# Hybrid S5 and stick-breaking layer: one weight sum of a Strassen-Winograd group moved to an adding DMA, and six more such groups

## The chip, the cores and the metric

The kernel runs on one core of one Trainium2 chip. The metric is the device time of one execution in microseconds (us), the median of several runs. A profiled execution of the same program gives the trace that is read here.

## The reference, cut to what matters

One layer for 256 positions of width 2048: a half feed-forward (FFN 1), a mixer (state space and attention), a second half feed-forward (FFN 2) and a per-layer embedding. All numbers are float32. The change touches the two feed-forwards only, each with its own weights:

```python
def swiglu(h, w_gate, w_up, w_down):
    return (jax.nn.silu(h @ w_gate) * (h @ w_up)) @ w_down
x = x + 0.5 * swiglu(rms_norm(x, ffn1_norm[i]), ffn1_w_gate[i], ffn1_w_up[i], ffn1_w_down[i])
```

The gate and up weights are 2048 x 5632 and the down weight is 5632 x 2048, so one FFN streams 138 MB of weights through the core for 256 rows of activations.

## The kernel before, in words

**Products in three passes.** TensorE multiplies float32r (a rounded form of float32). Each operand is split into a high part and a low rest, and a product is hi x hi, lo x hi and hi x lo, three matmuls of 128 x 128 by 128 x 512. A weight tile `raw` holds four K tiles of 128 rows by 512 columns (1 MB) and comes by a DMA of the SP queue; there are five such buffers. `split` (L181, L184) turns half of it, 128 x 1024 elements, into a pair: ScalarE casts the high part (`whi` or `shi`), VectorE subtracts to get the rest (`wlo` or `slo`).

**Plain blocks and columns.** `gemm_block` and `Seven.column` take a weight tile half by half: one pair and twelve matmuls (two K tiles, two row tiles of 128 positions, three passes) into two PSUM banks.

**Groups of seven.** `Seven.chunk` (L505) takes two weight tiles at once (in the gate and up stage one of `w_gate` and one of `w_up`, in the down stage two neighbouring column blocks) and forms a Strassen-Winograd product of 2 x 2 blocks. The weight blocks are b11 and b21 (the halves of the first tile) and b12 and b22 (the halves of the second). `Seven.add` (L500, recorded at L502) forms four sums on VectorE: t1 = b11+b12, t2 = t1+b22, t4 = t2+b21, t3 = b12+b22. `Seven.product` (L488, matmuls at L495, L496 and L498) splits one block or sum into a pair and does six matmuls. There are seven products with their own PSUM banks, 42 matmuls where two columns take 48. The matching sums of the activations (`sum_forms`, L459) are made once for each stretch of K.

**Where groups stand.** In the gate and up stage a block f is 512 columns of both weights and has K in four pieces kb = 0 to 3. The flag `two` (L605) chooses: with it, kb 0 and 1 are groups and kb 2 and 3 are columns; without it, only kb 0 is a group. In FFN 2, f = 0 is a plain pair and f = 1 to 10 alternate, starting with `two`. In FFN 1, f = 0 to 6 are plain (the preparation of the state-space part runs beside them), f = 7 (`early`) has one group, and f = 8, 9, 10 have two, one, two. The down stage has three groups in each FFN, by a written plan (L688). This makes 27 groups in all. After a block's last product `opened` and `gated` (L590, L595) fold the banks on VectorE, L621 adds the last one and `turned` transposes.

**The ring of pairs.** `weight_pair` (L284) hands out the buffers: four pairs `whi`/`wlo`, and while `ring` holds a pool, three more (`shi`/`slo`) in turn with them, seven in all. `sums_phase` (L294) fills `ring` when it opens: at the start of FFN 2, and before f = 7 in FFN 1.

**Order.** Each engine executes its own list in order. The order of the lists comes from the framework's planner, which may move an instruction ahead of others that it does not depend on; instructions inside `pin` keep their place. `step` and `put_off` run waiting work between groups of matmuls. SP issues the weight loads and the transposing copies `hT<-mid`; the queue of POOL (GpSimd) carries a few DMAs, among them `fetch_x` (L146, recorded at L150), which brings the residual back into two of the five `raw` buffers near the end of the gate and up stage.

Of the kernel before, what the change touches and what calls it, by code (L numbers as in the profile page):

```python
# [13 lines left out]
ALU = mybir.AluOpType  # L14
# [19 lines left out]
def layer_kernel(ctx: ExitStack, tc: tile.TileContext, a: dict, shapes: dict, out: bass.AP):  # L34
    nc = tc.nc
# [27 lines left out]
    def uid(s):  # L63
        count[0] += 1
        return f"{s}_{count[0]}"
# [4 lines left out]
    def com(tag):  # L70
        return get(comp, tag, *{"sg": (1024, 1), "h": (1024, 2), "sq": (NB, 1), "mid": (2048, 1)}[tag])

    def phase(name):
        return tc.tile_pool(name=name, bufs=1, reuse_waits="tile")
# [24 lines left out]
    def step():  # L99
        for g in list(beside):  # L100
            if next(g, beside) is beside:
                beside.remove(g)

    def finish(g):
        for _ in g:
            pass

    def put_off(steps, fn, *args):


        def g():
            for _ in range(steps):
                yield
            fn(*args)

        return start(g())
# [165 lines left out]
    ring = [None, 0]  # L282
# [10 lines left out]
    @contextmanager  # L293
    def sums_phase(name):  # L294
        with phase(name) as pool:
            ring[:] = [pool, 0]
            yield pool
            ring[0] = None

# [150 lines left out]
    def sum_forms(pool, u, kind="n"):  # L450

        sums = pool.tile([P, 2, NB], F32, tag="sum", name=uid("rows"), bufs=2)
        s = sums.rearrange("p j n -> p (j n)").rearrange("p (z j x b) -> p z j x b", z=4, j=2, b=32)
        (a11, a21), (a12, a22) = ([u[:, k : k + 2, 4 * t : 4 * t + 4] for t in range(TT)] for k in (0, 2))
        for z, (x, y, op) in enumerate((
            (a21, a22, ALU.subtract), (s[:, 0], a11, ALU.subtract),
            (a11, a21, ALU.subtract), (a12, s[:, 1], ALU.add),
        )):
            nc.vector.tensor_tensor(out=s[:, z], in0=x, in1=y, op=op)  # L459
        both = halves(kind)  # L460
        split(*both, sums.rearrange("p j n -> p (j n)").rearrange("p (z t) -> p z t", z=4))
        return both

    class Seven:
# [39 lines left out]

        def chunk(self, kb, final=()):  # L505

            raws = []
            for w, n0 in self.ws:
                raw = wp.tile([P, 4, NB], F32, tag="raw", name=uid("raw"), bufs=5)
                nc.sync.dma_start(  # L510
                    raw, w[4 * kb * P : 4 * (kb + 1) * P, n0 : n0 + NB].rearrange("(j p) n -> p j n", p=P)
                )
                raws.append(raw)
            b11, b21, b12, b22 = (raw[:, 2 * h : 2 * h + 2, :] for raw in raws for h in range(2))
            parts, sums = self.act(kb), self.sums(kb)

            def whole(k, t):
                return [[u[:, 2 * k + j, t * P : (t + 1) * P] for j in range(2)] for u in parts]

            def summed(z):  # L520
                return [[u[:, z, j * P : (j + 1) * P] for j in range(2)] for u in sums]

            self.product(1, whole(0, 0), b11, final)
            t1 = self.add(b11, b12)
            self.product(5, summed(0), t1, final)
            step()
            t2 = self.add(t1, b22)
            self.product(6, summed(1), t2, final)
            t4 = self.add(t2, b21)
            self.product(4, whole(1, 1), t4, final)  # L530
            step()
            t3 = self.add(b12, b22)
            self.product(7, summed(2), t3, final)
            self.product(2, whole(1, 0), b21, final)
            step()
            self.product(3, summed(3), b22, final)
            step()

        def column(self, side, kbs, final=False):
# [14 lines left out]
    def ffn(i, xn, nxt, bg=None):  # L554
# [3 lines left out]
        early = 7 if bg else 0  # L558
# [19 lines left out]
        for f in range(NF):  # L578
            if prep and f == early:
                finish(prep)  # L580
                side.close()
                prep = None
                sevens = pools.enter_context(sums_phase(f"sums{i}"))
                hp = pools.enter_context(phase(f"h{i}b"))
                sums = [sum_forms(sevens, whole_rows(sevens, xn(kb)), "h") for kb in range(2)]
            if sevens and f:
                sg, hh = com("sg"), com("h")
                gate_cols, up_cols = ([u[:, t * NB : (t + 1) * NB] for t in range(TT)] for u in (sg, hh))

                def opened(s, g=gate_cols, u=up_cols):  # L590
                    nc.scalar.copy(g[0], s.bank(1))
                    nc.vector.tensor_tensor(out=u[0], in0=s.bank(6), in1=g[0], op=ALU.add)
                    nc.vector.tensor_tensor(out=u[1], in0=s.bank(7), in1=u[0], op=ALU.add)

                def gated(s, g=gate_cols, u=up_cols, hh=hh):  # L595
                    for z, (ps, other) in enumerate(((s.bank(2), g[0]), (s.bank(4), u[1]))):
                        nc.vector.tensor_tensor(out=g[z], in0=ps, in1=other, op=ALU.add)
                        nc.scalar.activation(g[z], g[z], AF.Silu, scale=xn.rs(z))
                    v = hh.rearrange("p (t n) -> p t n", t=TT)
                    nc.vector.tensor_tensor(  # L600
                        out=v, in0=s.bank(5).unsqueeze(1).to_broadcast([P, TT, NB]), in1=v, op=ALU.subtract
                    )

                s = Seven(xn, lambda kb: sums[kb], ((wg, f * NB), (wu, f * NB)), sevens)
                two = f % 2 == (0 if bg else 1)  # L605
                if f == early:
                    s.column(0, (1, 2, 3))
                    s.chunk(0, (*shared, 2, 4))
                    put_off(0, opened, s)
                elif two:  # L610
                    s.chunk(0)
                    s.column(0, (2, 3))
                    s.chunk(1, (*shared, 2, 4))
                    put_off(0, opened, s)
                else:
                    s.chunk(0, shared)
                    put_off(0, opened, s)
                    s.column(0, (1, 2, 3), True)
                put_off(0, gated, s)
                s.column(1, (2, 3) if two and f != early else (1, 2, 3), True)  # L620
                nc.vector.tensor_tensor(out=hh, in0=s.banks[3.8], in1=hh, op=ALU.add)  # L621
                for t in range(TT):
                    nc.vector.scalar_tensor_tensor(  # L623
                        out=up_cols[t], in0=up_cols[t], scalar=xn.rs(t), in1=gate_cols[t], op0=ALU.mult, op1=ALU.mult
                    )
                put_off(2, turned, hp, f, hh)
                continue

            def gate():
                for t in range(TT):  # L630
                    nc.scalar.activation(sg[:, t * NB : (t + 1) * NB], pg[t], AF.Silu, scale=xn.rs(t))

            first = ()
            if f == 0 and bg:
                warm_up(10)
                first = first_quarters(wg, xn)
            if f == 0 and not bg:
                both = gemm_pair(xn, ((wg, 0), (wu, 0)), KD)
                pg = next(both)
                sums = [sum_forms(sevens, whole_rows(sevens, xn(kb))) for kb in range(2)]  # L640
            else:
                pg = gemm_block(xn, wg, f * NB, KD, first)
            sg = com("sg")
            if f == 0 and bg:
                for n in range(ND):
                    put_off(n, load_x, n)
                    put_off(n + 2, xn.squares, n)
                put_off(6, gate)
            else:
                gate()  # L650
            pu = gemm_block(xn, wu, f * NB, KD) if f or bg else next(both)
            if prep and f == 0:
                start(prep)
            hh = com("h")
            for t in range(TT):
                nc.vector.scalar_tensor_tensor(
                    out=hh[:, t * NB : (t + 1) * NB], in0=pu[t], scalar=xn.rs(t),
                    in1=sg[:, t * NB : (t + 1) * NB], op0=ALU.mult, op1=ALU.mult,
                )
            put_off(2, turned, hp, f, hh)  # L660
# [31 lines left out]
        for n in range(0, ND, 2):  # L692
# [17 lines left out]
            for u in plan:  # L710
                kb, final = int(u[1:]), u == plan[-1]
# [715 lines left out]
    pool = s5p.enter_context(phase("s5"))  # L1427
# [10 lines left out]
    pool = atp.enter_context(phase("attn"))  # L1438
# [105 lines left out]
    early, part, ms, root, r, tmp = (small(1) for _ in range(6))  # L1544
# [132 lines left out]
```

## Time and profile before

| What | us |
|---|---|
| median of 3 runs (lowest to highest) | 1849.53 (1849.49 to 1849.77) |
| profiled execution, its own time | 1849.49 |
| its span, first to last instruction | 1847.7 |
| PE (TensorE matmul) busy | 1835.4 |
| DVE (VectorE) busy | 1462.3 |
| ACT (ScalarE) busy | 1019.6 |
| POOL (GpSimd) busy | 62.1 |

The profiled execution took 1.8 us more than its span; this is what lies before the first and after the last instruction. Busy time of an engine is the union of its instructions. A matmul row lasts longer than the distance to the next one, because matmuls overlap, so the pace is read from start to start. The 16 DMA engines were busy 63.6% of the span with the queue of SP.

### The profile page before, as it was taken

The page shows a single profiled execution, that of the slowest core. Times are in us where ns is not written, and L with a number is a line of the kernel's source. Part 1 is how long each engine was busy: PE and PEld are TensorE (multiplying, and loading weights), DVE is VectorE, ACT ScalarE, POOL GpSimd, SP SyncE. Part 2 cuts the span into 40 slices and gives each one's busy share as a digit, 9 for nine tenths or more (in the row PEclk, how much of TensorE's full clock was granted, in tenths as well). Part 3 has the DMA queues.
Part 4 walks back from the last instruction along what each step waited for, and adds up shares of the span by engine and source line. Part 5 has one row for each costly group of instructions (what it writes and reads, how often), then busy time and mean ns, then how long its engine had stood idle before and what let it go on. Part 6 is the DMA issues. An engine that isn't in the chain of part 4 may idle for free. (4 is left out here: it accounts for less than half of the span.)

```text
span 1847.7 us, 23966 instructions
## 1 busy us (share of the span) xinstructions
PE 1835.4 (99%) x9032; PEld 1518.1 (82%) x9032; DVE 1462.3 (79%) x1718; ACT 1019.6 (55%) x1187; POOL 62.1 (3%) x108
## 2 busy tenths in 40 slices
PE   9999999999999999999999999999999999999998
PEld 7888887788888888888898888888888888888887
DVE  8967664999987976687566799989898998797655
ACT  7444444555565655365685465555555645565554
POOL 0011000000000000010021000000000000000000
PEclk9999999999999999999999999999999999999999
DMA  9888867567656566675636776675656585656563
GB/s 331 284 270 282 251 213 220 182 227 239 229 197 241 187 233 209 192 263 166 216 139 214 219 271 212 226 240 188 205 183 228 200 267 185 247 184 232 179 220 125
DMA packets 232308, 406.36 MB, mean 220 GB/s; under 512 B 26785, under 2 KB 50721, under 8 KB 231905
## 3 DMA queue, kind: packets, MB, share of 16 engines
q1 hardware_dynamic: 227824, 392.81, 63.6%
q0 software_dynamic: 3648, 10.62, 1.8%
q8 instruction: 70, 1.15, 0.3%
q10 hardware_dynamic: 720, 1.41, 0.2%
q14 instruction: 46, 0.37, 0.1%
HBM read 373.46 MB, written 11.93 MB: 209 GB/s over the span
## 5 line engine op out<-in xcount | busy, mean ns | idle before, releaser
L184 DVE TENSOR_TENSOR wlo<-raw,whi 128x1024 fp32r<-128x1024 f32 x473 | 572.3, 1221 | 215.8 <-ACT whi L181 207.4
L181 ACT CAST whi<-raw 128x1024 fp32r<-128x1024 f32 x473 | 491.6, 1051 | 400.6 <-PE acc L324 258.0
L323 PE MATMUL acc<-whi,nhi 128*128 128x512 f32 x1112 | 436.3, 392 | 1.6 <-ACT whi L181 1.6
L324 PE MATMUL acc<-whi,nlo 128*128 128x512 f32 x1112 | 433.2, 390 | 0.0
L328 PE MATMUL acc<-wlo,nhi 128*128 128x512 f32 x1112 | 304.2, 389 | 0.3 <-DVE wlo L184 0.2
L323 PEld LDWEIGHTS acc<-whi,nhi 128*128 128x128 f32 x1112 | 209.0, 188 | 47.1 <-ACT whi L181 2.4
L328 PEld LDWEIGHTS acc<-wlo,nhi 128*128 128x128 f32 x1112 | 208.6, 188 | 44.5 <-DVE wlo L184 1.2
L324 PEld LDWEIGHTS acc<-whi,nlo 128*128 128x128 f32 x1112 | 209.1, 188 | 42.4
L184 DVE TENSOR_TENSOR slo<-raw,shi 128x1024 fp32r<-128x1024 f32 x166 | 202.0, 1217 | 42.4 <-ACT shi L181 42.3
L181 ACT CAST shi<-raw 128x1024 fp32r<-128x1024 f32 x166 | 174.3, 1051 | 110.7 <-PE acc L324 33.4
L181 ACT CAST whi<-sum 128x1024 fp32r<-128x1024 f32 x61 | 64.2, 1053 | 96.8 <-DVE sum L502 80.9
L181 ACT CAST shi<-sum 128x1024 fp32r<-128x1024 f32 x47 | 49.4, 1052 | 72.7 <-DVE sum L502 56.2
L323 PE MATMUL acc<-whi,hhi 128*128 128x512 f32 x216 | 84.1, 389 | 0.0
L324 PE MATMUL acc<-whi,hlo 128*128 128x512 f32 x216 | 84.0, 389 | 0.0
L324 PE MATMUL aux<-whi,hlo 128*128 128x512 f32 x200 | 77.9, 390 | 0.6 <-DVE hlo L184 0.6
L323 PE MATMUL aux<-whi,hhi 128*128 128x512 f32 x200 | 77.8, 389 | 0.0
L184 DVE TENSOR_TENSOR wlo<-sum,whi 128x1024 fp32r<-128x1024 f32 x61 | 74.5, 1221 | 1.9 <-ACT whi L181 1.2
L184 DVE TENSOR_TENSOR hlo<-hT,hhi 128x1024 fp32r<-128x1024 f32 x56 | 68.1, 1217 | 5.9 <-ACT hhi L181 5.7
L181 ACT CAST hhi<-hT 128x1024 fp32r<-128x1024 f32 x56 | 58.7, 1049 | 15.4 <-PE aux L328 13.1
L502 DVE TENSOR_TENSOR sum<-sum,raw 128x1024 f32<-128x1024 f32 x54 | 66.0, 1221 | 1.0
L328 PE MATMUL acc<-wlo,hhi 128*128 128x512 f32 x216 | 65.7, 390 | 0.2 <-DVE wlo L184 0.2
L323 PE MATMUL acc<-shi,hhi 128*128 128x512 f32 x160 | 62.3, 389 | 0.0
(373 smaller groups left out, 3013.7 us busy)
## 6 DMA issues: line engine op xcount, KB each, us to landing
raw<-in_ffn_w_up SPq DMA_DIRECT2D x88, 1024.0 KB, 6.0
raw<-in_ffn_w_down SPq DMA_DIRECT2D x88, 1024.0 KB, 5.1
raw<-in_ffn_w_gate SPq DMA_DIRECT2D x86, 1024.0 KB, 7.0
raw<-in_w_in SPq DMA_DIRECT2D x32, 1024.0 KB, 5.9
raw<-in_w_out SPq DMA_DIRECT2D x16, 1024.0 KB, 5.3
raw<-in_w_ple_gate SPq DMA_DIRECT2D x16, 1024.0 KB, 5.1
hT<-mid SPq DMA_DIRECT2D x160, 64.0 KB, 4.3
h<-mid SPq DMA_DIRECT2D x176, 32.0 KB, 2.7
```

Of the source, the lines that this page charges most:

```text
L181: copy = nc.scalar.copy(hi, src)
L184: nc.vector.tensor_tensor(out=lo, in0=src, in1=hi.bitcast(F32), op=ALU.subtract)
L323: nc.tensor.matmul(ps[t], lhsT=lh, rhs=hi[:, j, cols], start=start and j == 0, stop=False)
L324: nc.tensor.matmul(ps[t], lhsT=ll, rhs=hi[:, j, cols], start=False, stop=False)
L328: nc.tensor.matmul(ps[t], lhsT=lh, rhs=lo[:, j, cols], start=False, stop=stop and j == 1)
L502: nc.vector.tensor_tensor(out=t, in0=x, in1=y, op=ALU.add)
```

## The change

Four things are edited. In `chunk`, t3 = b12+b22 is no longer made by VectorE: POOL issues a DMA that adds b22 to b12 in place (`accum_op`), after t1 has read b12, and product 7 splits b12 itself. The order of the products becomes 1, 5, 6, 4, 2, 3, 7 (it was 1, 5, 6, 4, 7, 2, 3), and t1 is made ahead of product 1. The flag `two` becomes true for every block after `early`: all ten blocks f = 1 to 10 of FFN 2, and f = 8, 9, 10 of FFN 1, have two groups, so there are 33 groups. `ring` is filled by the first group of an FFN instead of by `sums_phase`.

```diff
     def sums_phase(name):
         with phase(name) as pool:
-            ring[:] = [pool, 0]
             yield pool
             ring[0] = None
...
         def chunk(self, kb, final=()):
 
+            if ring[0] is None:
+                ring[:] = [self.pool, 0]
             raws = []
...
+            t1 = self.add(b11, b12)
+            nc.gpsimd.dma_start(b12, b22, accum_op=ALU.add)
             self.product(1, whole(0, 0), b11, final)
-            t1 = self.add(b11, b12)
             self.product(5, summed(0), t1, final)
             step()
             t2 = self.add(t1, b22)
...
             self.product(4, whole(1, 1), t4, final)
             step()
-            t3 = self.add(b12, b22)
-            self.product(7, summed(2), t3, final)
             self.product(2, whole(1, 0), b21, final)
+            self.product(3, summed(3), b22, final)
             step()
-            self.product(3, summed(3), b22, final)
+            self.product(7, summed(2), b12, final)
             step()
...
-                two = f % 2 == (0 if bg else 1)
+                two = f != early
```

## The prediction

> **What bounds the kernel now.** I read the page first, for the shares; then the busy time of each engine in the ten blocks f = 1 to 10 of FFN 2, where five of the six new groups go; then the waits of VectorE there, and single rows.
>
> ```profile
> span 1847.7 us, 23966 instructions
> PE 1835.4 (99%) x9032; PEld 1518.1 (82%) x9032; DVE 1462.3 (79%) x1718; ACT 1019.6 (55%) x1187; POOL 62.1 (3%) x108
> ```
>
> ```profile
> core 0: us, PE busy (x) PEld busy (x) DVE busy (x) ACT busy (x) POOL busy (x), PEclk, DMA share, GB/s
> 1088.70:1129.60 40.90, 40.90 (x182) 33.85 (x182) 40.53 (x40) 23.92 (x26) 0.00 (x0) 1.00 0.58 206
> 1129.60:1171.70 42.10, 42.10 (x187) 34.86 (x186) 34.94 (x34) 22.27 (x24) 0.00 (x0) 1.00 0.69 225
> ...
> 1378.60:1420.70 42.10, 41.80 (x184) 34.12 (x184) 34.06 (x33) 22.79 (x24) 0.00 (x0) 1.00 0.69 225
> 1420.70:1461.60 40.90, 40.90 (x182) 33.49 (x181) 39.98 (x39) 21.55 (x23) 0.00 (x0) 1.00 0.59 206
> 1461.60:1503.70 42.10, 41.91 (x184) 34.11 (x183) 38.18 (x40) 24.96 (x27) 4.33 (x8) 1.00 0.74 234
> sum 415.00, PE 414.51 PEld 341.79 DVE 377.80 ACT 226.82 POOL 4.33; mean PE 41.45 PEld 34.18 DVE 37.78 ACT 22.68 POOL 0.43
> ```
>
> Each window is one block: the 40.90 us ones have two groups, the 42.10 us ones one. PE is busy 414.51 of 415.00 us at clock 1.00, so TensorE bounds this stage and a matmul taken away is time taken away, as long as the pairs arrive. VectorE is the next bound: 40.53 of 40.90 us in a block with two groups, about 35 of 42.10 us in the next one, where it catches up.
>
> ```profile
> DVE sg L597 <- PE acc L328: 13.3, 8, 4.7
> DVE wlo L184 <- ACT whi L181: 9.9, 7, 3.2
> DVE h L621 <- PE aux L328: 8.2, 5, 4.5
> DVE slo L184 <- ACT shi L181: 2.5, 4, 1.4
> DVE hlo L184 <- ACT hhi L181: 1.2, 1, 1.2
> ```
>
> These waits (total, times, longest) make about 35 us of VectorE idle in the ten blocks, and 21.5 us of it are L597 and L621 waiting for PE to finish: VectorE is ahead there. That idle time is the room for more groups.
>
> **The change part by part.** *Fewer matmuls.* The pace of PE comes from two starts:
>
> ```profile
> 1088.74 0.39 PE L495 MATMUL acc<-whi,hhi 128*128 128x512 f32 x1
> 1094.18 0.39 PE L495 MATMUL aux<-whi,nhi 128*128 128x512 f32 x1
> ```
>
> The second is four products (24 matmuls) behind the first: 5.44 / 24 = 0.227 us each, 1.36 us for a product. A new group replaces two columns, 42 matmuls for 48, so it saves 1.36 us. Six groups (five in FFN 2, one in FFN 1's f = 9) save 36 matmuls, 6 x 1.36 = 8.2 us, all on the path.
>
> *VectorE.* Its pace also comes from starts:
>
> ```profile
> 1227.90 1.21 DVE L184 TENSOR_TENSOR slo<-raw,shi 128x1024 fp32r<-128x1024 f32 x1
> 1229.04 1.21 DVE L184 TENSOR_TENSOR wlo<-raw,whi 128x1024 fp32r<-128x1024 f32 x1
> 1230.17 1.21 DVE L184 TENSOR_TENSOR slo<-raw,shi 128x1024 fp32r<-128x1024 f32 x1
> 1231.31 1.21 DVE L184 TENSOR_TENSOR wlo<-raw,whi 128x1024 fp32r<-128x1024 f32 x1
> ```
>
> Three steps in 3.41 us are 1.14 us for an operation of 128 x 1024. A group had 7 subtractions and 4 sums; now it has 7 and 3. Two columns have 4 subtractions. In the ten blocks of FFN 2, 15 old groups lose one sum each and 5 new ones add 10 - 4 = 6 each: -15 + 30 = 15 operations, 17.1 us more. PE's time there becomes 415.0 - 5 x 1.36 = 408.2 us, VectorE's 377.8 + 17.1 = 394.9 us, 96.7% of it. For one block that is 39.5 us of VectorE under 40.8 us of PE: 1.3 us of room, where it was 3.7. It costs nothing while PE covers it, but the alternation of a tight and a loose block is gone. In a tight block of now VectorE idles only 0.4 to 0.9 us of 40.9 (40.53 and 39.98 busy), so it can run at 97%; none of these shows a PE gap in the rows above. The gaps are in the two loose ones that follow, 0.30 and 0.19 us, at the hand-over. I take 0.25 us for each of the ten blocks, 2.5 us, of which 0.5 is there already: **2.0 us** back.
>
> *ScalarE* gets 18 more casts of about 1 us; at 226.82 of 415.00 us it hides them.
>
> *The adding DMA.* The trace has no such DMA. The nearest rows are DMAs that POOL issues:
>
> ```profile
> L984 POOL DMA_DIRECT2D scr_m<-m x4 | 2.3, 572 | 42.3 <-DVE m L972 42.3
> scr_m<-m POOLq DMA_DIRECT2D x4, 512.0 KB, 4.8
> scr_x<-x POOLq DMA_DIRECT2D x8, 256.0 KB, 3.7
> x<-scr_x POOLq DMA_DIRECT2D x8, 256.0 KB, 7.9
> ```
>
> A plain copy of the same 512 KB takes 0.57 us of POOL and lands 4.8 us after its issue. The add also reads what it writes, three passes for two: 4.8 x 3/2 = 7.2 us, an estimate and my value. Far ends: 3.7 us, what half the bytes took, and 15.8 us, twice the 7.9 us of a 256 KB load that queued with seven others in the last window above (DMA share 0.74). What hides it is the work between t1 and the cast of product 7:
>
> ```profile
> 1242.92 1.22 DVE L502 TENSOR_TENSOR sum<-raw,raw 128x1024 f32<-128x1024 f32 x1
> ```
>
> ```profile
> 1252.70 1.05 ACT L181 CAST whi<-sum 128x1024 fp32r<-128x1024 f32 x1
> ```
>
> The first row is a t1, done at 1244.1; the second is the cast of t3 in the same group, 8.6 us later. There product 7 was fifth; now it is seventh, two subtractions later (+2.3 us) and one sum less (-1.1): 9.7 us. With 0.6 us for POOL, a landing within 9.1 us costs nothing; 7.2 us leaves 1.9. If it is late, ScalarE stops at that cast, the casts and subtractions behind it wait, and PE eats its pairs. Where it falls behind `fetch_x` in POOL's queue (eight DMAs, 4.33 us in the last window above) it is late once in each FFN. The added bytes, two groups of 0.5 MB written and 1 MB read on top of 8.4 MB a block, lift the DMA share from 0.6 to about 0.75: loads still fit, at nothing.
>
> In that estimate one rule of the Trainium skill speaks against the change. Under DMA: Bandwidth & Descriptors, section "Queues, rings and completion order", it says that each DMA engine goes round-robin between the queues that have work, packet by packet. So beside a weight load the add would get half of an engine; by this the sum would come out on the slow side, as in the second rival. The rows of 4.8 and 7.9 us do not settle it, and no run here shows the add itself.
>
> *Order and ring.* t1 ahead of product 1 delays that subtraction by 1.14 us, which the queued pairs cover. The first tile is freed one product sooner, the second as before, after the last. In f = 0 of FFN 2 there are now four pairs instead of seven, and there is one place where this counts:
>
> ```profile
> 1053.78 1.22 DVE L184 TENSOR_TENSOR wlo<-raw,whi 128x1024 fp32r<-128x1024 f32 x1
> 1064.07 1.23 DVE L184 TENSOR_TENSOR slo<-raw,shi 128x1024 fp32r<-128x1024 f32 x1 [9.07 <-ACT shi L181]
> ```
>
> ```profile
> 1062.98 1.05 ACT L181 CAST shi<-raw 128x1024 fp32r<-128x1024 f32 x1 [9.77 <-DMA raw<-in_ffn_w_gate]
> ```
>
> ```profile
> 1066.98 0.39 PE L323 MATMUL acc<-shi,nhi 128*128 128x512 f32 x1
> ```
>
> A load is late and the pairs in stock carry PE from 1055 to 1067, where the cast done at 1064.0 is used: 3.0 us to spare. With four pairs the last casts ahead of the gap wait for PE, some 3.4 us, their tile is freed and perhaps refilled that much later: 0.4 us lost. Bounds: 0 (the load waits for something else) and 3.4. In FFN 1 the column ahead of its first group loses the three pairs too; there PE waits already:
>
> ```profile
> PE acc L328 <- DVE slo L184: 2.2, 1, 2.2
> PE aux L495 <- ACT shi L181: 0.9, 1, 0.9
> ```
>
> A new order may take these 3.1 us away or double them; I take 0.
>
> **Sum.** 1849.5 (profiled; the median is 1849.53) - 8.2 + 2.0 + 0.4 = **1843.7 us**.
>
> **The rivals.** *Hand-overs eat the gain.* With 1.3 us of room in each block, L597 and L621 stand in VectorE's list ahead of subtractions that PE needs. For it: FFN 1 lost 3.1 us at one such place. Against: the tight blocks above lose nothing. At 0.7 us for a block, 13 blocks lose 9 us and the time is 1849.5 - 8.2 + 9 = 1850, no change.
>
> *The add lands late.* Past 9.1 us each us is VectorE idle time twice in a block. The room is 1.3 us and the gain on the old mean block (41.5 to 40.8) 0.7, so it decides from 1.0 us late, a landing of 10.1 us. At 10.6 us (1.5 late) a block is 39.5 + 3.0 = 42.5 us, 1.7 over PE; 13 blocks give 22 us: 1843.7 + 22 = **1866 us**, slower. Were it to share every DMA engine half and half with the loads, it would land at 2 x 7.2 = 14.4 us, 5.3 late, and cost 13 x 9.3 = 121 us (0.05 of the 0.26 below). For it: 7.9 us for half the bytes under load. Against: 4.8 us for the same bytes, and the planner can put column work ahead of product 7.
>
> *VectorE starves POOL.* POOL's issues took 0.54 us each (4.33 us for eight) in a window where VectorE was 38.18 of 42.10 busy, so nothing of this is seen. It would act as the late add and is counted there.
>
> By the Trainium skill, SBUF — State Buffer, section "SBUF: two separate sides", POOL cannot write a DMA's descriptors while VectorE runs in a mode that takes both ports; for operations with two SBUF inputs, as here, the lock holds only against POOL operations that read SBUF. The trace agrees (0.54 us).
>
> **How the numbers follow.** Forecast 0.58, hand-overs 0.16, late add 0.26. What a measurement here can tell from no change is about 0.2%, 3.7 us: 1845.8 to 1853.2. Faster is the forecast, same the hand-overs, slower the late add. The low end is 1849.5 - 8.2 - 3.1 + 1.2 = 1839.4, with FFN 1's waits gone and half of the 2.4 us of costs; the high end is the late add's 1866, beyond which lies about half of that case.
>
> **What would show it.** Right: 8996 PE instructions and about 415 - 6.8 = 408 us for the ten blocks, with PE gaps of some 2 us; VectorE at 95% or more of them and its waits on L597 and L621 nearly gone; the adding DMA landing under 9 us. Wrong: ScalarE or VectorE waiting for a DMA that writes `raw` from `raw`, or PE waiting for L184 at every hand-over.

## The result and the profile after

The changed kernel takes 1838.22 us (median of 6 runs, 1837.90 to 1839.51); the kernel before took 1849.60 us beside it (6 runs, 1849.26 to 1849.77). The ratio is 0.994 (95% interval 0.9927 to 0.9953), so it is faster by 11.4 us. The forecast was 5.8 us, and the range ended at 1839.4, 1.2 us short of the result. The profiled execution took 1838.15 us with a span of 1836.3.

The page of the changed kernel, the lines on the engines, the queue and the adding DMA (behind the edit of `sums_phase` the line numbers are one lower than before, behind `chunk` one higher: the sum is L501, the matmuls of a group are L494, L495 and L497, those of a column L322, L323 and L327):

```profile
span 1836.3 us, 24143 instructions
PE 1824.7 (99%) x8996; PEld 1511.5 (82%) x8996; DVE 1471.9 (80%) x1727; ACT 1035.6 (56%) x1205; POOL 92.0 (5%) x141
q0 software_dynamic: 8400, 27.92, 6.8%
L525 POOL DMA_DIRECT2D raw<-raw x33 | 28.7, 869 | 856.8 <-DVE sum L501 459.4
raw<-raw POOLq DMA_DIRECT2D x33, 512.0 KB, 5.8
```

PE has 8996 matmuls, 36 fewer, as counted. VectorE has nine operations more (27 sums gone, 6 x 6 added). POOL takes 0.87 us to issue an adding DMA, and the median one lands 5.8 us after its issue.

The changed kernel's busy time by block, f = 1 to 10 of FFN 2, the same stage as in the prediction:

```profile
core 0: us, PE busy (x) PEld busy (x) DVE busy (x) ACT busy (x) POOL busy (x), PEclk, DMA share, GB/s
1085.10:1125.90 40.80, 40.80 (x182) 33.78 (x181) 39.88 (x39) 25.09 (x27) 1.71 (x2) 1.00 0.78 235
1125.90:1166.70 40.80, 40.80 (x182) 33.78 (x181) 38.28 (x38) 24.70 (x26) 1.75 (x2) 1.00 0.84 255
...
1411.50:1452.30 40.80, 40.80 (x182) 33.80 (x181) 40.08 (x40) 24.74 (x27) 1.75 (x2) 1.00 0.74 232
1452.30:1493.10 40.80, 40.80 (x182) 33.80 (x181) 35.60 (x37) 23.14 (x25) 5.23 (x9) 1.00 0.81 246
sum 408.00, PE 408.00 PEld 337.73 DVE 389.05 ACT 237.92 POOL 20.83; mean PE 40.80 PEld 33.77 DVE 38.90 ACT 23.79 POOL 2.08
```

All ten blocks are alike now: 40.80 us each, PE busy in all of it, VectorE 389.05 of 408.00 us (95.4%). The hand-over gaps are not there. The longest waits of VectorE in the same stretch (total, times, longest):

```profile
DVE slo L184 <- ACT shi L181: 6.6, 5, 3.5
DVE wlo L184 <- ACT whi L181: 5.1, 7, 1.2
DVE h L593 <- PE aux L497: 4.0, 3, 2.2
```

The 21.5 us that VectorE waited for PE to finish a column are gone. What it still waits for PE, 4.0 us, is at L593, for the last matmul of a group.

**Where the 11.4 us are.** A busy share hides short stalls here, because a matmul row lasts 0.39 us and the next one starts after 0.227. Starts do not hide them. So I mark four places in the program by the first matmul of a group there: the first group of FFN 1, the first group of its block f = 10, the first group of FFN 2, and the first group behind its ten blocks (it is in the down stage, with four columns ahead of it). Before (the first of FFN 2 stands in the prediction, at 1088.74):

```profile
335.39 0.39 PE L495 MATMUL acc<-whi,nhi 128*128 128x512 f32 x1
446.81 0.39 PE L495 MATMUL acc<-whi,nhi 128*128 128x512 f32 x1
1526.90 0.39 PE L495 MATMUL acc<-shi,hhi 128*128 128x512 f32 x1
```

After:

```profile
332.91 0.39 PE L494 MATMUL acc<-whi,nhi 128*128 128x512 f32 x1
443.78 0.39 PE L494 MATMUL acc<-shi,nhi 128*128 128x512 f32 x1
1085.18 0.39 PE L494 MATMUL acc<-whi,hhi 128*128 128x512 f32 x1
1515.02 0.39 PE L494 MATMUL acc<-whi,hhi 128*128 128x512 f32 x1
```

The lead is 2.5 us at the first group of FFN 1, 3.0 at its block f = 10, 3.6 at the first group of FFN 2 and 11.9 behind the ten blocks; at the end of the span it is 11.4. From mark to mark the ten blocks went from 438.16 to 429.84 us, 8.3 us, of which five groups explain 6.8. Another 1.5 us are stalls that before had there, although its PE showed only 0.49 us of idle time. In FFN 1 the new group, the second of block f = 9, explains 1.4 of 3.0 us, and 2.5 us were gained before that group was reached. So 3.2 of the 11.4 us, more than a quarter, are not matmuls.

### The profile page after: what moved, and what is told of

The parts are those of the page before. It is cut to its first block, busy times and chain, and to the rows that moved or that the text cites. A ratio compares the mean times of both kernels' runs of the same rounds, so it can differ in the third digit from the quotient of the medians.

```text
span 1836.3 us, 24143 instructions
## 1 busy us (share of the span) xinstructions
PE 1824.7 (99%) x8996; PEld 1511.5 (82%) x8996; DVE 1471.9 (80%) x1727; ACT 1035.6 (56%) x1205; POOL 92.0 (5%) x141
## 3 DMA queue, kind: packets, MB, share of 16 engines
q0 software_dynamic: 8400, 27.92, 6.8%
## 4 chain that ended last, share of the span: by engine, by line
PE 94%; DVE 2%; DMA 2%; ACT 1%; issue 0%; SPq 0%; ACTq 0%; DVEq 0%
PE acc L322 18%; PE acc L323 18%; PE acc L327 18%; PE aux L327 7%; PE aux L322 7%; PE aux L323 7%; PE acc L497 3%; PE acc L494 3%; PE acc L495 3%; PE aux L494 2%; PE aux L497 2%; PE aux L495 2%; DMA raw<-in_ffn_w_gate 1%; DVE wlo L184 1%; DMA raw<-in_w_in 1%; ACT whi L181 0%
## 5 line engine op out<-in xcount | busy, mean ns | idle before, releaser
L184 DVE TENSOR_TENSOR wlo<-raw,whi 128x1024 fp32r<-128x1024 f32 x497 | 602.4, 1223 | 224.2 <-ACT whi L181 218.5
L181 ACT CAST whi<-raw 128x1024 fp32r<-128x1024 f32 x497 | 517.0, 1051 | 400.0 <-PE acc L323 272.7
L322 PE MATMUL acc<-whi,nhi 128*128 128x512 f32 x1132 | 443.6, 392 | 2.5 <-ACT whi L181 1.6
L323 PE MATMUL acc<-whi,nlo 128*128 128x512 f32 x1132 | 440.8, 389 | 0.0
L327 PE MATMUL acc<-wlo,nhi 128*128 128x512 f32 x1132 | 309.7, 389 | 0.2 <-DVE wlo L184 0.2
L322 PEld LDWEIGHTS acc<-whi,nhi 128*128 128x128 f32 x1132 | 212.5, 188 | 49.0 <-ACT whi L181 2.9
L327 PEld LDWEIGHTS acc<-wlo,nhi 128*128 128x128 f32 x1132 | 212.4, 188 | 44.7 <-DVE wlo L184 0.6
L323 PEld LDWEIGHTS acc<-whi,nlo 128*128 128x128 f32 x1132 | 212.6, 188 | 43.2
L181 ACT CAST shi<-sum 128x1024 fp32r<-128x1024 f32 x42 | 44.3, 1054 | 74.0 <-DVE sum L501 72.2
L501 DVE TENSOR_TENSOR sum<-sum,raw 128x1024 f32<-128x1024 f32 x66 | 80.5, 1220 | 0.4
L322 PE MATMUL acc<-whi,hhi 128*128 128x512 f32 x204 | 79.4, 389 | 0.0
L323 PE MATMUL acc<-whi,hlo 128*128 128x512 f32 x204 | 79.4, 389 | 0.0
L525 POOL DMA_DIRECT2D raw<-raw x33 | 28.7, 869 | 856.8 <-DVE sum L501 459.4
L322 PE MATMUL aux<-whi,hhi 128*128 128x512 f32 x176 | 68.5, 389 | 0.0
L323 PE MATMUL aux<-whi,hlo 128*128 128x512 f32 x176 | 68.5, 389 | 0.0
L327 PE MATMUL acc<-wlo,hhi 128*128 128x512 f32 x204 | 61.5, 389 | 0.0
```

What stands on the lines that cost most here:

```text
L181: copy = nc.scalar.copy(hi, src)
L184: nc.vector.tensor_tensor(out=lo, in0=src, in1=hi.bitcast(F32), op=ALU.subtract)
L322: nc.tensor.matmul(ps[t], lhsT=lh, rhs=hi[:, j, cols], start=start and j == 0, stop=False)
L323: nc.tensor.matmul(ps[t], lhsT=ll, rhs=hi[:, j, cols], start=False, stop=False)
L327: nc.tensor.matmul(ps[t], lhsT=lh, rhs=lo[:, j, cols], start=False, stop=stop and j == 1)
L501: nc.vector.tensor_tensor(out=t, in0=x, in1=y, op=ALU.add)
```

## The experiments

The theory after the result: the six groups are worth their 8.2 us, and the rest comes from VectorE, which gets 27 operations less work in the old groups and so catches up where PE used to wait. Rivals: the rest comes from the new order of products and its `ring`; or VectorE doesn't matter and two groups a block would have been won without the DMA. The kernels ran in four sets, each set on one chip, and the kernel before, beside them, took 1850.19, 1850.08, 1850.15 and 1850.13 us. Where starts are given they are those of the four places above, from each kernel's own trace.

**The parts one by one.** Two groups a block, with t3 still on VectorE:

```diff
-                two = f % 2 == (0 if bg else 1)
+                two = f != early
```

> The kernel before with the new flag alone: 33 groups, all four weight sums on VectorE, old product order, old ring. Theory (the adding DMA is what makes room): a block of FFN 2 with two groups needs 39.5 + 2 x 1.14 = 41.8 us of VectorE against 40.8 us of PE; with the 0.4 to 0.9 us that VectorE idles in a tight block it becomes the bound at about 42.3 us, so ten blocks lose 15 us to PE's 408 and the time is 1849.6 - 8.2 + 15 = 1856 us. Rival (VectorE had room enough, the DMA does nothing for the time): 1849.6 - 8.2 = 1841 us.

Measured: 1854.14 us (1851.31 to 1859.10), ratio 1.0023 (1.0013 to 1.0032), slower. A stretch of eight blocks of FFN 2:

```profile
1170.00:1506.00 336.00, 329.23 (x1444) 269.55 (x1443) 330.26 (x317) 188.82 (x203) 4.36 (x8) 1.00 0.65 213
```

and PE's longest waits in the whole span:

```profile
PE acc L495 <- ACT whi L181: 4.0, 2, 2.0
PE acc L328 <- DVE slo L184: 2.2, 1, 2.2
PE acc L495 <- ACT shi L181: 2.0, 1, 2.0
```

VectorE is at 98.3% and PE falls to 98.0%: VectorE sets the pace. The matmuls that were taken away come back as waits for pairs: the ten blocks take 438.97 us from mark to mark, 9.1 more than with the DMA. The rival falls.

The DMA and the order of products, with the old flag and the old ring:

```diff
     def sums_phase(name):
         with phase(name) as pool:
+            ring[:] = [pool, 0]
...
-            if ring[0] is None:
-                ring[:] = [self.pool, 0]
...
-                two = f != early
+                two = f % 2 == (0 if bg else 1)
```

> The changed kernel with the old flag and the old ring: 27 groups, the adding DMA and the new product order. No matmul goes, so only stalls of PE can. Theory (room in VectorE ends the stalls at hand-overs): FFN 2's 1.4 us of PE stalls go, FFN 1's stay: 1848.2 us. Rival (the stalls come from the order of the lists and the ring, not from VectorE's load): 1849.6 us within 0.5. Second rival (late adds cost): above 1850 us.

Measured: 1847.53 us (1846.29 to 1848.27), ratio 0.9986 (0.9976 to 0.9995): 2.7 us gained with no matmul removed. The ten blocks take 436.56 us, 1.6 less than before's 438.16.

The new ring alone, in the kernel before:

```diff
     def sums_phase(name):
         with phase(name) as pool:
-            ring[:] = [pool, 0]
...
+            if ring[0] is None:
+                ring[:] = [self.pool, 0]
```

> The kernel before with the ring filled by the first group instead of at the start of the phase, nothing else. Theory (the ring alone ends the 2.2 us stall ahead of FFN 1's first group, because VectorE then no longer stands behind a block's last sum with casts piled up ahead of it): 1849.6 - 2 = 1847.6 us. Rival (the stall went because VectorE has less to do there): no change, 1849.6 us. My prediction's step (four pairs instead of seven at the start of FFN 2 lose 0.4 us): 1850.0 us.

Measured: 1849.37 us (1848.85 to 1850.32), ratio 0.9996 (0.9987 to 1.0006), no difference. The gain that I expected is there and is lost again: the first group of FFN 1 starts at 333.1 us (335.4 before), the one in block f = 10 at 446.7 (446.8 before). The ten blocks take 438.41 us, as before.

The changed kernel with the old ring:

```diff
     def sums_phase(name):
         with phase(name) as pool:
+            ring[:] = [pool, 0]
...
-            if ring[0] is None:
-                ring[:] = [self.pool, 0]
```

> The changed kernel with the ring filled at the start of the phase again. Theory (the ring ends FFN 1's stall): 1838.2 + 2 = 1840.2 us, with PE waiting some 2 us for L184 near 320 us. Rival (less VectorE work ends it): 1838.2 us, no wait there.

Measured: 1842.80 us (1839.13 to 1844.27), ratio 0.9957 (0.9941 to 0.9974). So the ring is worth about 4 us in the changed kernel (by the median of four runs that lie 5 us apart) and nothing that can be measured in the one before. The wait of 2.2 us at the entry of FFN 1 is back, and the ten blocks take 432.1 us for 429.8.

What the ring does at the entry of FFN 1 can be read in VectorE's rows. Before:

```profile
316.50 1.41 DVE L656 SCALAR_TENSOR_TENSOR h<-acc,sm,sg 128x512 f32<-128x512 f32 x2 [6.53 <-PE acc L328]
321.28 1.22 DVE L184 TENSOR_TENSOR slo<-raw,shi 128x1024 fp32r<-128x1024 f32 x1
```

```profile
322.55 0.73 PE L328 MATMUL acc<-slo,nhi 128*128 128x512 f32 x2 [2.24 <-DVE slo L184]
```

After:

```profile
311.53 1.23 DVE L184 TENSOR_TENSOR wlo<-raw,whi 128x1024 fp32r<-128x1024 f32 x1 [1.50 <-ACT whi L181]
316.56 1.41 DVE L657 SCALAR_TENSOR_TENSOR h<-acc,sm,sg 128x512 f32<-128x512 f32 x2 [3.81 <-PE acc L327]
319.11 2.32 DVE L184 TENSOR_TENSOR wlo<-raw,whi 128x1024 fp32r<-128x1024 f32 x2
```

Before, VectorE stood idle for 6.5 us ahead of L656, which needs the last matmul of block 6, while casts of the next block were done, and the `slo` that PE waits for at 322.55 was ready only then (321.28 is its start). With four pairs one subtraction (311.53) stands ahead of that operation in VectorE's list, and PE does not wait there.

**The add itself.** The changed kernel once more:

> The changed kernel unchanged, as the yardstick on this chip for the other three. Every theory: 1838 us, 11.4 us under the kernel before.

Measured: 1838.92 us (1838.57 to 1839.61), ratio 0.9939 (0.9922 to 0.9955). ScalarE waited for the add 16.8 us in 9 waits.

The same without the DMA (product 7 reads b12 alone, t3 is left out):

```diff
-            nc.gpsimd.dma_start(b12, b22, accum_op=ALU.add)
```

> The changed kernel without the adding DMA and without the sum: product 7 splits b12 as it was loaded, so the sum t3 is left out of the computation. What differs from the changed kernel is the price of the DMA itself. Theory (adds land in a median of 5.8 us, inside the cover, except a few): 1837 us, the 1.1 us that PE waits in FFN 1 near 426 us gone. Rival (late adds and added DMA traffic are what keeps the kernel from more): under 1834 us.

Measured: 1837.14 us (1836.46 to 1837.54), ratio 0.9929 (0.9914 to 0.9944). The DMA costs 1.8 us in all. By starts it is one place. In the changed kernel the second group of f = 9 in FFN 1, which is the new one, and the first of f = 10, at 443.78, start 22.1 us apart:

```profile
421.69 0.39 PE L494 MATMUL acc<-whi,nhi 128*128 128x512 f32 x1
```

Without the add they are 20.4 us apart (421.92 and 442.32), as such groups are in the ten blocks. The rows of the changed kernel at that place:

```profile
414.20 1.22 DVE L501 TENSOR_TENSOR sum<-raw,raw 128x1024 f32<-128x1024 f32 x1
416.10 0.87 POOL L525 DMA_DIRECT2D raw<-raw  x1 [18.01 <-DVE sum L501]
424.75 1.05 ACT L181 CAST shi<-raw 128x1024 fp32r<-128x1024 f32 x1 [5.98 <-DMA raw<-raw]
425.71 1.04 ACT L181 CAST whi<-sum 128x1024 fp32r<-128x1024 f32 x1
```

```profile
426.80 0.50 PE L494 MATMUL acc<-whi,nhi 128*128 128x512 f32 x1 [0.87 <-ACT whi L181]
```

The add was issued at 416.10 and landed 8.5 us later. The cast of product 7 stands on ScalarE ahead of the cast of t4 here, although the code makes product 7 last: the order of an engine's list is the scheduler's. PE waits for t4's cast, which is queued behind the one that waits for the DMA. In the changed kernel's second trace, that of the repeat above, the same two groups are again 22.1 us apart, and the ten blocks lose 0.6 us more than in the first.

The add issued twice, so that it lands later (product 7 then gets b12 + 2 b22):

```diff
             nc.gpsimd.dma_start(b12, b22, accum_op=ALU.add)
+            nc.gpsimd.dma_start(b12, b22, accum_op=ALU.add)
```

> The changed kernel with the same add issued twice, the second waiting for the first, so that b12 becomes b12 + 2 b22 (product 7 has another operand). The landing becomes about 2 x (0.9 + 5.8) = 13.3 us behind t1. My prediction's pricing (9.7 us of cover, then every us late is VectorE idle twice in a block): 3.6 us late, 39.5 + 7.2 = 46.7 us for a block, 13 x 5.9 = 77 us, 1915 us. Rival (the planner's other work and the pairs in stock carry PE past a late cast): under 1850 us.

Measured: 1917.34 us (1914.42 to 1920.18), ratio 1.0363 (1.0348 to 1.0378). ScalarE's waits for it:

```profile
ACT whi L181 <- DMA raw<-raw: 78.8, 15, 10.4
ACT shi L181 <- DMA raw<-raw: 68.2, 12, 10.0
```

The rival of the late add is real, 147 us of waiting in 27 waits, and 78 us more than the changed kernel. It only needs a landing that late. That the expected 1915 us came so near is in part luck: it was worked out with a cover of 9.7 us, and the next kernel shows that the cover is shorter.

Product 7 moved back to fifth, where before had it:

```diff
             step()
+            self.product(7, summed(2), b12, final)
             self.product(2, whole(1, 0), b21, final)
-            self.product(3, summed(3), b22, final)
             step()
-            self.product(7, summed(2), b12, final)
+            self.product(3, summed(3), b22, final)
```

> The changed kernel with product 7 back in its old place, fifth, ahead of products 2 and 3: the cover of the add shrinks by two subtractions, 2.3 us, to 7.4 us. Theory (median landing 5.8 + 0.9 = 6.7 us, so that only the slower half, up to 9.2 us, comes late, by 1 us in the mean of those): about 13 us of VectorE idle over 26 groups, half of it inside the room: 1842 us. Rival (place does not matter, the planner shifts it anyway): 1838 us.

Measured: 1874.13 us (1873.32 to 1874.18), ratio 1.0129 (1.0113 to 1.0144); both expectations missed it by far. ScalarE's waits for the add:

```profile
ACT shi L181 <- DMA raw<-raw: 40.2, 9, 6.4
ACT whi L181 <- DMA raw<-raw: 27.2, 11, 5.0
```

and one group of it:

```profile
1150.11 1.22 DVE L501 TENSOR_TENSOR sum<-raw,raw 128x1024 f32<-128x1024 f32 x1
...
1151.98 0.87 POOL L525 DMA_DIRECT2D raw<-raw  x1 [23.50 <-DMA hT<-mid]
...
1157.44 1.05 ACT L181 CAST whi<-raw 128x1024 fp32r<-128x1024 f32 x1 [2.69 <-DMA raw<-raw]
```

Without the wait the cast would have started at 1154.75, 3.4 us after t1's end at 1151.33. By the prediction's way of counting it would be 9.7 less two subtractions (2.3), 7.4 us. The cast that waits for an add's landing can be told in 31 groups of each trace: it was ready 3.4 us after t1's end in the median here and 7.8 us in the changed kernel, while the add landed 7.0 and 6.4 us after it. So the place in the code cost 4.4 us of cover, not 2.3, and the move of product 7 to the end is what makes the DMA affordable: it is worth 35 us. In this kernel 50.6 us more of ScalarE's waiting (67.4 for 16.8) cost 35.2 us, in the one with two adds 130 us cost 78.4: 0.6 to 0.7 us of time for each us of it.

**Where the gain without matmuls comes from.** The kernel before with t3 left out, nothing else changed:

```diff
-            t3 = self.add(b12, b22)
-            self.product(7, summed(2), t3, final)
+            self.product(7, summed(2), b12, final)
```

> The kernel before without its sum t3: product 7 splits b12 as it was loaded, so that sum is left out of the computation; no DMA, old product order, old ring, 27 groups. It takes 1.14 us of VectorE work from each group and nothing else. Theory (VectorE's load inside the groups made the stalls at hand-overs): the 1.4 us of PE stalls in FFN 2 go, some of FFN 1's too: 1847.5 us, like the kernel with the add alone (1847.5). Rival (the new product order did it): 1850 us, no change.

Measured: 1847.55 us (1846.32 to 1848.67), ratio 0.9985 (0.9976 to 0.9994): the same 2.6 us as the DMA with its order gave. So it is the sum that VectorE no longer makes, and neither the DMA nor the order; the ten blocks take 436.56 us here too. Leaving out t3 also spares the cast of product 7 its wait for that sum, which no run separates from the freed 1.14 us; in the kernel with the add that cast had the DMA to wait for instead, at the same gain.

The changed kernel with the old flag, thus 27 groups, the add, the order and the ring:

```diff
-                two = f != early
+                two = f % 2 == (0 if bg else 1)
```

> The changed kernel with the old flag only: 27 groups, the adding DMA, new order, new ring. Theory (the ring's 2.3 us ahead of FFN 1's first group are kept once VectorE has room, and were given back 70 us later in the kernel with the ring alone): 1847.5 - 2.3 = 1845.2 us; six groups more (8.2 us) then make 1838 with a loss of 1 us. Rival (ring and add do not add up): 1847.5 us.

Measured: 1844.35 us (1844.03 to 1845.25), ratio 0.9969 (0.9958 to 0.9981): 5.8 us with all the old matmuls. Its starts at the last two places:

```profile
1084.46 0.39 PE L494 MATMUL acc<-whi,hhi 128*128 128x512 f32 x1
...
1521.02 0.39 PE L494 MATMUL acc<-shi,hhi 128*128 128x512 f32 x1
```

Its ten blocks take 436.56 us, 1.6 less than before's 438.16, and that is 1926 matmuls at 0.2267 us, with nothing left for stalls; the changed kernel's 429.84 are 6.7 less again, the price of five groups (6.8). In FFN 1 it leads before by 3.4 us at block f = 10, where the changed kernel, with one group more and 1.4 us of matmuls less, leads by 3.0: that group's 1.4 us went to the late add.

Two groups in block f = 7 of FFN 1 too, and then one more group in each half of the down stage as well:

```diff
-                    s.column(0, (1, 2, 3))
-                    s.chunk(0, (*shared, 2, 4))
+                    s.column(0, (2, 3))
+                    s.chunk(0)
+                    s.chunk(1, (*shared, 2, 4))
...
-                s.column(1, (2, 3) if two and f != early else (1, 2, 3), True)
+                s.column(1, (2, 3) if two or f == early else (1, 2, 3), True)
```

> The changed kernel with two groups in block f = 7 of FFN 1 as well (the columns of kb 2 and 3 first, then both groups): 34 groups, 1.36 us of matmuls less. Theory (VectorE has room, PE is the bound): 1838.5 - 1.4 = 1837.1 us. Rival (VectorE is full there, since the activations' sums are made at the same time): 1840 us, with PE waiting for ScalarE or VectorE between 320 and 360 us.

Measured: 1847.76 us (1847.04 to 1851.15), ratio 0.9989 (0.9980 to 0.9998), 8.8 us more than the changed kernel, for one group that saves 1.4. The start of FFN 1 in this kernel:

```profile
320.00:340.00 20.00, 16.34 (x60) 12.16 (x59) 19.77 (x24) 9.87 (x10) 0.90 (x1) 0.83 0.37 92
```

The same 20 us in the changed kernel, and the next:

```profile
320.00:340.00 20.00, 18.64 (x82) 15.03 (x81) 19.83 (x24) 10.55 (x12) 0.91 (x1) 1.00 0.59 184
340.00:360.00 20.00, 20.00 (x89) 16.54 (x89) 19.94 (x20) 11.94 (x13) 0.88 (x1) 1.00 0.90 289
```

VectorE is full in all of them. It also makes the sums of the activations there, so there is no room for a group. Part of the 8.8 us is the clock: behind a wait of 2.6 us PE's granted clock was 0.50 from 333.0 to 339.2, and matmuls started 0.43 us apart where it is 0.227 elsewhere; eight such steps alone are 1.6 us. Block f = 7 is also where the ring's gain was lost for the most part when it was alone, 1.6 of 2.3 us (the lead at f = 8 is 0.7): VectorE bounds the start of FFN 1.

The second kernel, with the plans of `down_groups` below on top of that one:

> As early_two, with one more group in each half of the down stage (four more, 38 in all): 5 x 1.36 = 6.8 us of matmuls less than the changed kernel. In the down stage VectorE is about 80% busy, but only three weight buffers are free there, and a group holds two until its add has landed. Theory (room of VectorE decides): 1838.5 - 6.8 + 1 = 1833 us. Rival (the weight buffers decide, loads come late by the add's 6 us): 1841 us or more, with ScalarE waiting for the down weights.

Measured: 1841.92 us (1841.44 to 1843.99), ratio 0.9957 (0.9940 to 0.9974): the down stage gives back 5.8 us of what block 7 loses. The time is the one that the rival expected, but not for its reason: the four groups are worth what their matmuls take.

**What was still open.** It was not known yet whether ring and freed VectorE together make the 5.8 us, without the DMA and the new order, and whether more is to be had. The kernel before with t3 left out and the new ring:

```diff
-            ring[:] = [pool, 0]
...
+            if ring[0] is None:
+                ring[:] = [self.pool, 0]
...
-            t3 = self.add(b12, b22)
-            self.product(7, summed(2), t3, final)
+            self.product(7, summed(2), b12, final)
```

> The kernel before without its sum t3 (left out of the computation) and with the new ring: 27 groups, no DMA, old product order. Alone the ring gave 0.8 us and the missing sum 2.6. Theory (the ring's 2.3 us ahead of FFN 1's first group stay only where VectorE has room behind it, so the two together give more than their sum): 1844.3 us, like the kernel with add, ring and 27 groups (1844.35). Rival (they just add up): 1846.8 us. Second rival (the new product order is needed too): 1846 us or more.

Measured: 1845.32 us (1844.75 to 1845.43), ratio 0.9973 (0.9962 to 0.9984), 4.8 us gained. Alone the two gave 2.6 and 0.8, and the second is no clear difference, so the times alone do not settle whether they add. The starts do: at block f = 10 the missing sum alone leads by 1.3 us, the ring alone by 0.1, the two together by 3.1 (443.7). The ring brings the first group of FFN 1 forward by 2.5 us (332.9), and only with less work on VectorE is the lead kept. The kernel with the add and the new order gained 1.0 us more; whether the order is worth that stays open.

Four more groups in the down stages, one more in each of their halves, so 37:

```diff
-            ("c2", "c3", "s0", "c4", "c5", "c6", "s1", "c7", "c8", "c9", "c10"),
-            ("c1", "c2", "s0", "c3", "c4", "a5"),
+            ("c2", "c3", "s0", "c4", "c5", "s1", "c6", "c7", "s8", "c9", "c10"),
+            ("c1", "s0", "c2", "c3", "s4", "a5"),
```

> The changed kernel with one more group in each half of the down stage of both FFNs, four more, 37 in all, and FFN 1's block 7 as it was. 4 x 1.36 = 5.4 us of matmuls go. Theory (VectorE, not the weight buffers, is what a group needs, and the down stage has 20% of it free): 1838.5 - 5.4 = 1833.1 us. Rival (the weight buffers decide): 1837 us or more, with ScalarE waiting longer for the down weights.

Measured: 1835.67 us (1834.79 to 1837.59), ratio 0.9924 (0.9909 to 0.9938), the fastest of all, some 3 us below the changed kernel for 5.4 us of matmuls, and between the two expectations. The down stages of this kernel:

```profile
500.00:690.00 190.00, 188.47 (x829) 155.01 (x828) 173.07 (x180) 120.34 (x133) 4.36 (x5) 1.00 0.71 227
1500.00:1690.00 190.00, 190.00 (x840) 157.34 (x839) 175.62 (x184) 120.22 (x132) 4.36 (x5) 1.00 0.71 230
```

VectorE is at 91 to 92% and PE is idle for 1.5 us in the first, in two waits of 0.8 us for the pair of an activation (`hhi`, `hlo`). The rival's sign is there as well: ScalarE waits 50.1 us for the down weights, 25.1 in the changed kernel, but PE shows no wait for them. Its profile, of the slowest of its four runs, shows another loss of 1.4 us in block f = 9 of FFN 1, the place of the late add (the group of f = 10 starts at 445.2 us, 443.8 in the changed kernel).

Two more groups in the first halves of these stages, 39:

```diff
-            ("c2", "c3", "s0", "c4", "c5", "s1", "c6", "c7", "s8", "c9", "c10"),
+            ("c2", "s0", "c3", "c4", "s1", "c5", "s6", "c7", "s8", "c9", "c10"),
```

> As down_groups with a fourth group in the first half of the down stage (39 in all): 8.2 us of matmuls less than the changed kernel. Theory: 1838.5 - 8.2 + 0.5 = 1831 us. Rival (four groups within eleven pieces leave VectorE no room there, as with two groups in FFN 1's block 7): 1834 us or more, with PE waiting in the down stage.

Measured: 1841.61 us (1840.29 to 1843.87), ratio 0.9955 (0.9941 to 0.9970), 5.9 us worse than with 37. In 1500 to 1690 us:

```profile
1500.00:1690.00 190.00, 187.06 (x810) 152.29 (x809) 181.20 (x191) 122.19 (x135) 5.27 (x6) 0.99 0.71 228
```

VectorE at 95.4% as in the ten blocks of FFN 2, but here PE loses 2.9 us. A share alone is no limit; where the groups stand counts. Why the same share is covered in one stage and not in the other was not tried.

## Why the forecast was wrong, step by step

- **Fewer matmuls, -8.2 us: right.** From 27 to 33 groups with everything else equal, the five in FFN 2 brought 6.7 us for 6.8. The sixth, in FFN 1, brought its 1.4 and lost it to the late landing of its own add.
- **The failed step is the term of the stalls: "I take 0.25 us for each of the ten blocks", 2.0 us back.** The ten blocks gave 1.5 us instead. I carried the gaps of the old loose blocks over to new blocks, without asking what the missing sum does to the cause of these gaps. All four kernels with 27 groups that take t3 off VectorE, with and without the add, the new order and the ring, need 436.56 us for these blocks and have no stall left; with t3 on VectorE and the new ring it is 438.41. So the missing sum ended the gaps. That VectorE was late because it came out of a block with two groups is my reading of it. I also read the gaps as 0.30 and 0.19 us, from idle time; by starts the three blocks f = 8 to 10 lose 0.7, 0.2 and 0.7 us, and the 0.2 is in a tight block, where I saw none.
- **"A new order may take these 3.1 us away or double them; I take 0": it took them away, a second term that was put at nothing.** With the old flag the lead at block f = 10 of FFN 1 is 3.4 us. Its cause can be named: four pairs let a subtraction pass ahead of VectorE's long wait (2.5 us), and the freed VectorE keeps that lead. The changed kernel gives 1.7 of it back to the late add.
- **Ring in f = 0 of FFN 2, 0.4 us lost: not seen.** From the last group of FFN 1 to the first of FFN 2 it is 461.9 us, 462.4 before; but the kernels with the new ring lie between 461.6 and 462.4 there and those with the old one between 461.9 and 462.8, so 0.4 us cannot be told. On the whole the sign was wrong too: the changed kernel with the old ring is 4 us slower. Of these, 2.3 lie in the ten blocks; by what path the ring acts there stays open.
- **Sum by measured terms:** -8.2 matmuls, -1.5 stalls of the ten blocks, -3.4 stalls of FFN 1, +1.7 late add, and -0.5 and +0.5 between and behind the stages: -11.4. The low end of my range had FFN 1's waits gone, but still 1.2 us of costs in it; a range that allowed the new stalls to be negative would have held the time.
- **VectorE at 96.7%: near.** 95.4% by the windows. Fifteen more operations at 1.14 us would be 17.1 us, and the windows show 11.3, as part of that work lies beyond their edges: 376 operations start in them, 366 before, ten more and not fifteen (the whole span has the nine operations more that were counted).
- **The adding DMA, landing 7.2 us and cover 9.7: both too long, and the errors offset, which is luck.** Its landings:

```profile
DMA to landing us min/median/max: 4.5/5.8/9.2
```

 The cover was shorter, too. In the changed kernel, a t1 and the cast that waited for its add:

```profile
1177.78 1.22 DVE L501 TENSOR_TENSOR sum<-raw,raw 128x1024 f32<-128x1024 f32 x1
...
1188.17 1.06 ACT L181 CAST shi<-raw 128x1024 fp32r<-128x1024 f32 x1 [1.29 <-DMA raw<-raw]
```

 The cast was ready 7.9 us after t1's end at 1179.00, close to the median of 7.8 us, and in FFN 1 at 418.77, 3.4 us after it. I took the distance from one group and supposed that the code's order holds on ScalarE.
- **Half of each DMA engine, by the Trainium skill's DMA: Bandwidth & Descriptors, "Queues, rings and completion order":** by the way I used it, a landing of 14.4 us. The 33 adds landed in 4.5 to 9.2 us with the DMA share at 0.74 to 0.86 in the ten blocks. The measurement decides against my use of the rule; it does not show that the engines do not take turns, since the sharing itself is in no row.
- **VectorE starves POOL: no.** 0.87 us an issue with VectorE busy for 95%, 0.30 more than the plain copy's 0.57; no issue took over 0.91 us in the rows read.
- **The two rivals:** the hand-overs did not come: PE idles nowhere in the ten blocks, although VectorE's room there is short (1.9 us a block, 1.3 forecast). The late add came with an effect on PE in one group of 33, one landing was past the 9.1 us named as free, and it is a threat at once when the landing or the cover moves by 4 us or more.

## What to carry to other kernels

When a change takes work off the second-busiest engine, ask of every stall in the trace whether that engine was late because of the work that goes; such stalls may go with it, as here, and a forecast that keeps them as a constant is then too cautious. Read stalls of a pipelined engine from the distance of starts at fixed places in the program, not from its idle time. Before moving an operation onto a DMA, find where its consumer really stands in its engine's list: the distance in the code is not the cover.

## What the runs showed of the hardware

- An adding DMA within SBUF of 512 KB took POOL 0.87 us to issue and landed after 5.8 us (median of 33), beside 0.57 and 4.8 us for a plain copy of the same size into a scratch buffer outside SBUF (`scr_m`) in the kernel before. Queue q0 grew from 10.62 to 27.92 MB and from 1.8% to 6.8% of 16 engines' span. That is 17.3 MB in 5.0% of 16 x 1836 us, or 44.5 us of engine time for an add, 11.8 GB/s for an engine; POOL's plain DMAs of before come to 10.62 MB in 532 us, 20 GB/s. These are estimates from the shares of the page.
- In the kernel with two groups in block 7, the granted clock fell to 0.83 in the 20 us where PE was busy for only 16.34 us; within them it was 0.50 from 333.0 to 339.2 us, with 0.43 us from matmul to matmul for 0.227. The kernel with the down stage's groups on top showed the same 0.83 there (16.66 us busy). It was 1.00 in the same window of the changed kernel.
